# One encoder layer on one core: order of the first products, of RWKV's steps and of the attention's value transposes

## The chip, the cores and the metric

The kernel runs on one core of a Trainium2 chip. The metric is the time of one execution in microseconds of device time. The kernel before was run three times.

## The reference

One encoder layer over 512 tokens of 1024 channels, in float32:

```python
h = rms_norm(x, mix_norm_g)
proj = h @ w_in
y_a = short_conv_mixer(proj[SC])
y_b = stick_breaking_attention(q, k, v)
y_c = rwkv7_mixer(proj[RW])
y_d = spatial_gating(proj[SG])
gates = sigmoid(proj[GATE] + gate_b)
merged = sum over a, b, c, d of gate * (y @ out)
x = x + merged @ w_o
h = rms_norm(x, ffn_norm_g)
x = x + conv_glu_ffn(h, w_up, ffn_conv_w, w_down)
return rms_norm(x, final_norm_g)
```

RWKV needs, for each token and head, `kk / max(sqrt(sum(kk * kk)), 1e-12)` and a sum over `r * k * r_k`: two sums over the channels of a head. The attention has four heads of 64 with `z = q k / 8`, a causal mask, `log_sigmoid` and a suffix sum.

## The kernel before

Every large product is made of three matmuls (`mm3`, L168: lines 169, 170, 171), since each fp32 operand is held as a high part (a rounded cast) and a low part (the rest): high by high, low by high, high by low. Weights come from HBM in pieces of 128x512 (`load_piece`, L107 to L118), issued by SP. `split` (L99) makes ACT cast the high part `whi` (L100) and DVE subtract for the low part `wlo` (L101); for the first four pieces POOL subtracts. A unit (`col_unit`) is 256 columns of a weight, four pieces, 16 groups of three matmuls for all 512 tokens. PSUM has four banks with the tag "mm" for the products and four with the tag "wk" for everything else.

The program on TensorE, in order: the input's norm, whose scale is put on the diagonal of a matrix (L282) that multiplies x (L287); the first three units of w_in (columns RW0+768, then RW0+256 with RW0, then RW0+512), the first two in halves of 256 tokens (`gemm2_halves`, L341); the short convolution's columns, the gating unit's, RWKV's later work with gate columns; then q, k and v of the attention, the gates with the attention between them, the output products, and the FFN. ACT, DVE and TensorE take their instructions in a fixed order that is known when the kernel is built: in the first part ordered by hand, later by a scheduler, and it does not change at run time.

Side work is written as Python generators in four threads ("norm", "rw", "rw1", "sg"). After every group of three matmuls `mm3` calls `tick`, which lets each thread go on once its count has run out; `yield n` means to come back n groups later. The constants YA to YH, Y1, YS, WN, WN2 are such counts. `rwkv_half` (L397) runs in "rw" for the first two heads and in "rw1" for the others. Its steps that matter here: lora products (L420, L422); ACT's sigmoids; the scan `cs`; the gate product (L434) and the first head sum (`head_sum`, L416) of `sq`, whose result `ssm` (L441) goes through Ln (L448) and Exp (L449) on ACT; the head sum of `rk` after YA groups, whose parts `qH`, `qL` come from `split`; later the masks `Dm` (L541), built through a DRAM copy, and their first product (L552). The state step S is at L639 and L641. "sg" does the layer norm of the gating unit.

The attention: v is copied (`vT`, L906), transposed by TensorE in four pieces (L909), cast (`vS`, L914) and subtracted (L879). The generator `attention` then makes z in three "wk" banks (L932 to L934), and after Y1 groups issues Abs (L941), Exp (L942), Ln (L943), DVE's addition (L945) and `spH`, `spL`; YE groups later come the suffix sums (L953), Exp (L957), and YF groups later the products with vS (L965).

Of the kernel before, what the change touches and what calls it, by code (L numbers as in the profile page):

```python
# [31 lines left out]

YA, YB, YC, YD, YE, YF, YG, YH = 6, 16, 32, 20, 15, 5, 11, 3
Y1 = 3
YS = 2
WN = 19
WN2 = 5
ND = 3
# [10 lines left out]
def hybrid_encoder_layer(  # L49
# [44 lines left out]
    sp.dma_start(out=g_row, in_=mix_norm_g[0].rearrange("(k p) -> k p", p=P))  # L94
# [81 lines left out]

    def half_of(hf):
        return slice(512 * hf, 512 * hf + 512)
# [4 lines left out]
    def norm_factor(ss):  # L183
        s1 = small.tile([P, 1], F32, tag="s1", name="s1")
        vec.tensor_tensor(out=s1, in0=ss[:, 0:1], in1=ss[:, 1:2], op=ALU.add)
# [42 lines left out]

    def mix_stats(tt):
        ss, sq, _ = norm_start(npool)  # L230
        for hf in range(2):
            norm_sums(ss, x0[tt], sq, hf)
        mix_rs[tt] = norm_factor(ss)
# [8 lines left out]
    wslots[:] = [(npool, 4, 4)] * 4  # L242
    first = col_unit(w_in_v, RW0 + 768, get=load_piece)
    wslots[:] = [(wA, NRA, NWA)] * NWA
    u_first = [hl for _, hl in first]
    load_x(2)
    load_x(3)
    second = col_unit(w_in_v, RW0 + 256, RW0, get=load_piece)
    u_second = [hl for _, hl in second]

# [27 lines left out]
    with tc.manual_schedule(engines={mybir.EngineType.PE, mybir.EngineType.Activation, mybir.EngineType.DVE}):  # L278
        for tt in range(2):
            mix_stats(tt)  # L280
# [9 lines left out]
        s0 = mix_gain(0, 0)  # L290
        split(*first[0][0], pool)
        split(*first[1][0], pool)
        act.copy(s0[1], s0[0])
        s1 = mix_gain(1, 0)
        split(*first[2][0], pool)
        split(*first[3][0], pool)
        vec.tensor_tensor(out=s0[2], in0=s0[0], in1=s0[1].bitcast(F32), op=ALU.subtract)
        split(*s1)
        s0, s1 = mix_gain(0, 1), mix_gain(1, 1)
        split(*s0)  # L300
        split(*s1)
        for tt in range(2, 4):
            mix_stats(tt)
# [14 lines left out]
    spawn("norm", mix_rest())  # L318
    for raw_hi_lo, _ in second:
        split(*raw_hi_lo)  # L320

# [25 lines left out]

    def gemm2_halves(units, between):

        ps = [[bank(), bank()] for _ in units]  # L350
        for t2_ in range(2):
            t_ = slice(256 * t2_, 256 * t2_ + 256)
            for u, pu in zip(units, ps):
                for ci, kt in [(ci, kt) for h in range(4) for ci in range(2) for kt in range(2 * h, 2 * h + 2)]:
                    hi, lo = u[kt // 2]
                    cs = slice(ci * P, (ci + 1) * P)
                    mm3(pu[ci][:, t_], hi[:, kt % 2, cs], lo[:, kt % 2, cs], hH[:, kt, t_], hL[:, kt, t_], kt == 0, kt == KT - 1)
            if t2_ == 0:
                between()
        return ps  # L360
# [36 lines left out]
    def rwkv_half(j, lora, xg, zk, zr, zv):  # L397

        while j == 1 and stage[0] < 1:
            yield 1  # L400
# [30 lines left out]
        head_sum = parts_of(sq)  # L431
        yield 3
        pg = bank("wk")
# [242 lines left out]

    pz, pz2 = gemm2_halves([u_first, u_second], lambda: (finish("norm"), spawn("norm", turn_vectors())))
    finish("norm")
# [215 lines left out]
    for j in range(2):  # L894
        ps = pss2[j]
        ks = apool.tile([P, 2, T], F32R, tag="kS", name="kS", bufs=2)
        for hp in range(2):
            own, oth = HS[hp], HS[1 - hp]
            act.copy(ks[own, hp, :], ps[own, :])
            lo_of(ks[oth, hp, :], ps[own, :], ks[own, hp, :])  # L900
        kS.append(ks)
    pss2 = gemm2(col_unit(w_in_v, SB0 + 512))
    for j in range(2):
        ps = pss2[j]
        v = apool.tile([P, T], F32, tag="vT", name="vT", bufs=2)
        act.copy(v, ps)  # L906
        pt = bank("wk")
        for s in range(4):
            pe.transpose(out=pt[:, s * P:(s + 1) * P], in_=v[:, s * P:(s + 1) * P], identity=ident)  # L909
        vs = apool.tile([P, 2, NT, P], F32R, tag="vS", name="vS", bufs=2)  # L910
        for hp in range(2):
            own, oth = HS[hp], HS[1 - hp]
            src = pt.rearrange("p (s c) -> p s c", s=4)[:, :, own]
            act.copy(vs[:, hp, :, own], src)  # L914
            lo_of(vs[:, hp, :, oth], src, vs[:, hp, :, own])
        vS.append(vs)

# [232 lines left out]
```

## Time and profile before

| what | us |
|---|---|
| median of three runs | 870.81 |
| lowest, highest | 870.16, 874.03 |
| the profiled execution | 871.75 |
| its span in the trace | 870.0 |
| TensorE busy | 852.2 |
| DVE busy | 510.1 |
| ACT busy | 414.0 |
| POOL busy | 18.9 |
| mean granted clock of TensorE | 0.996 of full speed |

The sum of a prediction is made against the profiled execution, because all durations come from it. A wait in the list of waits is time in which the engine had its next instruction and could not start it.

### The profile page before, as it was taken

Reading aid. Unit: us, or ns where it says so; the run is one execution under the profiler, and the core shown is the slowest. Engines: PE = TensorE matmul, PEld = TensorE weight load, DVE = VectorE, ACT = ScalarE, POOL = GpSimd, SP = SyncE. Lnnn points to the kernel's source line nnn. Section 1 sums busy time; section 2 is a strip of 40 time slices with the busy share of each in tenths; the row PEclk is TensorE's granted clock in tenths of the full one; section 3 lists DMA queues with packets and bytes.
Section 4 is the critical chain, followed back from the end, with each engine's and each line's share of the span. In section 5 each row is a group of like instructions: output and inputs, shape, how many; then the busy total and the mean of one; then the engine's idle time right before and its main releaser. Section 6 shows DMA issues by size and latency. Waiting matters only on the chain.

```text
span 870.0 us, 12669 instructions
## 1 busy us (share of the span) xinstructions
PE 852.2 (98%) x4767; PEld 706.0 (81%) x4767; DVE 510.1 (59%) x872; ACT 414.0 (48%) x676; POOL 18.9 (2%) x61
## 2 busy tenths in 40 slices
PE   6999999999999999999999999999999999999997
PEld 6978877788778888888888888888888888888886
DVE  5577757875364655555556676635665366634645
ACT  6474344743343587774345554413444154412425
POOL 6000000000000000000000000000000000000000
PEclk9999999999999999999999999999999999999999
DMA  7233241134123322226338153313433063311102
GB/s 240 60 94 91 83 112 40 60 92 109 50 75 97 98 72 73 73 73 206 97 94 262 45 159 108 97 38 128 125 97 86 7 197 98 97 38 60 49 1 97
DMA packets 102773, 82.20 MB, mean 94 GB/s; under 512 B 12716, under 2 KB 92152, under 8 KB 102712
## 3 DMA queue, kind: packets, MB, share of 16 engines
q1 hardware_dynamic: 102040, 79.82, 30.8%
q10 hardware_dynamic: 592, 1.31, 0.4%
q8 instruction: 37, 0.61, 0.3%
q0 software_dynamic: 80, 0.26, 0.1%
q14 instruction: 24, 0.20, 0.1%
HBM read 78.88 MB, written 2.49 MB: 94 GB/s over the span
## 4 chain that ended last, share of the span: by engine, by line
PE 90%; DVE 3%; ACT 2%; DMA 2%; issue 1%; POOL 1%; POOLq 0%; ACTq 0%; SPq 0%
PE mm L169 25%; PE mm L171 24%; PE mm L170 24%; PE wk L171 3%; PE wk L170 3%; PE wk L169 3%; PE wk L552 1%; PE wk L953 1%; PE wk L965 1%; DMA raw<-in_w_down_dram 1%; PE wk L496 1%; ACT sq L181 0%; DVE ib L531 0%; DMA x<-in_x_dram 0%; POOL wlo L101 0%
## 5 line engine op out<-in xcount | busy, mean ns | idle before, releaser
L100 ACT CAST whi<-raw 128x512 fp32r<-128x512 f32 x276 | 168.9, 621 | 292.5 <-PE mm L170 168.2
L101 DVE TENSOR_TENSOR wlo<-raw,whi 128x512 fp32r<-128x512 f32 x272 | 185.3, 688 | 155.5 <-ACT whi L100 153.1
L169 PE MATMUL mm<-hH,whi 128*128 128x512 f32 (+1 forms) x448 | 173.8, 388 | 1.0 <-ACT hH L100 0.9
L171 PE MATMUL mm<-hH,wlo 128*128 128x512 f32 (+1 forms) x448 | 169.4, 378 | 3.6 <-POOL wlo L101 3.6
L170 PE MATMUL mm<-hL,whi 128*128 128x512 f32 (+1 forms) x448 | 169.1, 378 | 0.9 <-DVE hL L101 0.9
L169 PE MATMUL mm<-h2H,whi 128*128 128x512 f32 (+1 forms) x368 | 140.0, 381 | 0.6 <-ACT h2H L100 0.6
L170 PE MATMUL mm<-h2L,whi 128*128 128x512 f32 (+1 forms) x368 | 139.9, 380 | 0.5 <-DVE h2L L101 0.5
L171 PE MATMUL mm<-h2H,wlo 128*128 128x512 f32 (+1 forms) x368 | 139.8, 380 | 0.0
L171 PEld LDWEIGHTS mm<-hH,wlo 128*128 128x128 f32 x448 | 85.5, 191 | 19.4 <-POOL wlo L101 3.8
L169 PEld LDWEIGHTS mm<-hH,whi 128*128 128x128 f32 x448 | 85.5, 191 | 18.5 <-issue 1.5
L170 PEld LDWEIGHTS mm<-hL,whi 128*128 128x128 f32 x448 | 85.5, 191 | 15.0 <-DVE hL L101 1.3
L169 PEld LDWEIGHTS mm<-h2H,whi 128*128 128x128 f32 x368 | 69.2, 188 | 13.9 <-ACT h2H L100 0.8
L170 PEld LDWEIGHTS mm<-h2L,whi 128*128 128x128 f32 x368 | 69.2, 188 | 13.9 <-DVE h2L L101 0.7
L171 PEld LDWEIGHTS mm<-h2H,wlo 128*128 128x128 f32 x368 | 69.2, 188 | 13.0
L171 PE MATMUL mm<-whi,aL 128*128 128x512 f32 (+1 forms) x92 | 35.5, 386 | 0.0
L169 PE MATMUL mm<-whi,aH 128*128 128x512 f32 (+1 forms) x92 | 35.4, 385 | 0.0
L170 PE MATMUL mm<-wlo,aH 128*128 128x512 f32 (+1 forms) x92 | 35.4, 385 | 0.0
L171 PE MATMUL wk<-whi,aL 128*128 128x512 f32 (+1 forms) x88 | 33.8, 384 | 0.0
L170 PE MATMUL wk<-wlo,aH 128*128 128x512 f32 (+1 forms) x88 | 33.8, 384 | 0.0
L169 PE MATMUL wk<-whi,aH 128*128 128x512 f32 (+1 forms) x88 | 33.8, 384 | 0.0
L1063 DVE SCALAR_TENSOR_TENSOR ga<-mm,vecs,ga 128x511 f32<-128x511 f32 x22 | 16.5, 750 | 29.3 <-ACT ga L1062 29.3
L1031 DVE TENSOR_TENSOR xt<-xt,mm 128x512 f32<-128x512 f32 x16 | 11.0, 688 | 31.7 <-PE mm L171 31.7
(346 smaller groups left out, 1198.8 us busy)
## 6 DMA issues: line engine op xcount, KB each, us to landing
raw<-in_w_in_dram SPq DMA_DIRECT2D x104, 256.0 KB
raw<-in_w_up_dram SPq DMA_DIRECT2D x176, 128.0 KB
raw<-in_w_down_dram SPq DMA_DIRECT2D x44, 256.0 KB
raw<-in_w_o_dram SPq DMA_DIRECT2D x16, 256.0 KB
x<-in_x_dram SPq DMA_DIRECT2D x4, 512.0 KB
raw<-in_w_in_dram SPq DMA_DIRECT2D x16, 128.0 KB
xt<-in_x_dram SPq DMA_DIRECT2D x4, 512.0 KB
out_dram<-xn SPq DMA_DIRECT2D x4, 320.0 KB
```

The source lines that it names most:

```text
L100: act.copy(hi, src)
L101: eng.tensor_tensor(out=lo, in0=src, in1=hi.bitcast(F32), op=ALU.subtract)
L169: pe.matmul(ps, lhsT=sh, rhs=mh, start=first, stop=False)
L170: pe.matmul(ps, lhsT=sh, rhs=ml, start=False, stop=False)
L171: pe.matmul(ps, lhsT=sl, rhs=mh, start=False, stop=last)
L496: pe.matmul(pgs[hp][:, q * P:(q + 1) * P], lhsT=lt, rhs=rh, start=True, stop=True)
L552: pe.matmul(ps[us, i * 64:i * 64 + 64], lhsT=lt, rhs=rh, start=True, stop=True)
L953: pe.matmul(reg, lhsT=lt, rhs=s_[:, OFF[sj]:OFF[sj] + W[sj]], start=False, stop=(sj == 3 and n == 1), skip_group_check=True)
L965: pe.matmul(po[:, si * P:T], lhsT=vS[j][:, hp, si, :], rhs=a_[:, cols], start=(si == 0 and n == 0), stop=(si == 3 and n == 1))
L1031: vec.tensor_tensor(out=xt[:, tt, half_of(hf)], in0=xt[:, tt, half_of(hf)], in1=bk, op=ALU.add)
L1063: vec.scalar_tensor_tensor(out=t0[:, 1:T], in0=ps[:, 0:T - 1], scalar=ffc(1, i), in1=t0[:, 1:T], op0=ALU.mult, op1=ALU.add)
```

## The change

- g_row is loaded by a DMA on ACT's queue, ahead of x. The first norm squares a row tile of 1024 columns in one instruction.
- The low parts of the first four pieces are made by DVE in a written order; `split` has no engine argument any more.
- The loads are ordered: x tiles 0 and 1, the first unit, the upper half of the second unit's rows, x tile 2, the rest of the second unit, x tile 3, the third unit. The third unit joins the first two: all three for the first 256 tokens (the first two in quarters, the third on two "wk" banks), then all three for the second 256.
- `rwkv_half` of the first heads starts 8 groups later (Y0). YN (5, was 3) stands ahead of the gate product, YP (5, was 3) ahead of P2, YC is 36 for 32, YS 3 for 2, WN 20, WN2 10.
- The value transposes with their casts become a generator `turn_values` in thread "sg", spawned after the attention, that starts after YV = 4 groups.

```diff
-YA, YB, YC, YD, YE, YF, YG, YH = 6, 16, 32, 20, 15, 5, 11, 3
+YA, YB, YC, YD, YE, YF, YG, YH = 6, 16, 36, 20, 15, 5, 11, 3
 Y1 = 3
-YS = 2
-WN = 19
-WN2 = 5
+YS = 3
+YN = 5
+YV = 4
+YP = 5
+Y0 = 8
+WN = 20
+WN2 = 10
...
-    def split(src, hi, lo, eng=vec):
+    def lo_of(src, hi, lo):
+        vec.tensor_tensor(out=lo, in0=src, in1=hi.bitcast(F32), op=ALU.subtract)
+
+    def split(src, hi, lo):
         act.copy(hi, src)
-        eng.tensor_tensor(out=lo, in0=src, in1=hi.bitcast(F32), op=ALU.subtract)
+        lo_of(src, hi, lo)
...
-    load_x(2)
-    load_x(3)
-    second = col_unit(w_in_v, RW0 + 256, RW0, get=load_piece)
+    second = col_unit(w_in_v[:, 0:KT // 2], RW0 + 256, RW0, get=load_piece)
+    load_x(2)
+    second += col_unit(w_in_v[:, KT // 2:KT], RW0 + 256, RW0, get=load_piece)
+    load_x(3)
+    wslots[:] = [(npool, 8, 8)]
+    third = col_unit(w_in_v, RW0 + 512, get=load_piece)
...
+        s0 = mix_gain(0, 0)
+        act.copy(s0[1], s0[0])
+        lo_of(*w[0])
+        s1 = mix_gain(1, 0)
+        act.copy(s1[1], s1[0])
+        lo_of(s0[0], s0[1], s0[2])
+        lo_of(s1[0], s1[1], s1[2])
+        lo_of(*w[1])
+        ss2 = mix_sums(2)
+        split(*w[2])
+        split(*w[3])
...
+    def first_units():
+
+        u = [[hl for _, hl in w] for w in (first, second, third)]
+        ps = [[bank(), bank()], [bank(), bank()]]
+        for hs in ((0, 1), (2, 3)):
+            for n in range(2):
+                gemm2_part(u[n], ps[n], 0, hs)
+        finish("norm")
+        ps.append([bank("wk"), bank("wk")])
+        gemm2_part(u[2], ps[2], 0)
+        spawn("norm", turn_vectors())
+        for hs in ((0, 1), (2, 3)):
+            for n in range(3):
+                gemm2_part(u[n], ps[n], 1, hs)
         return ps
...
+    vT = []
     for j in range(2):
-        ps = pss2[j]
         v = apool.tile([P, T], F32, tag="vT", name="vT", bufs=2)
-        act.copy(v, ps)
-        pt = bank("wk")
...
+        act.copy(v, pss2[j])
+        vT.append(v)
+
+    def turn_values():
+        yield YV
+        for j in range(2):
+            pt = bank("wk")
+            for s in range(4):
+                pe.transpose(out=pt[:, s * P:(s + 1) * P], in_=vT[j][:, s * P:(s + 1) * P], identity=ident)
...
     spawn("rw", attention())
+    spawn("sg", turn_values())
```

In the changed kernel the lines are some tens further on: a cast of `split` is L110 and a subtraction L107; Ln and Exp of `ssm` are L493 and L494.

ACT round RWKV's first head sum, before (gT is the gate product's copy, `y` the tile that Ln and Exp write, qH the high part of rk):

```order
L444 ACTIVATE wp<-cs 128x8x64
L446 ACTIVATE wm<-cs 128x512
L436 COPY gT<-wk 128x512
L100 CAST qH<-rk 128x512
L448 ACT_TABLE_LOAD
L448 ACTIVATE y_772<-ssm 128x512
L100 CAST whi<-raw 128x512
L449 ACT_TABLE_LOAD
L449 ACTIVATE y_772<-y_772 128x512
```

The same in the changed kernel, where scb is a copy of the short convolution's columns:

```order
L517 COPY var<-zv 128x4x2x64
L481 COPY gT<-wk 128x512
L110 CAST whi<-raw 128x512
L493 ACT_TABLE_LOAD
L493 ACTIVATE y_838<-ssm 128x512
L797 COPY scb<-mm 128x512
L494 ACT_TABLE_LOAD
L494 ACTIVATE y_838<-y_838 128x512
L110 CAST qH<-rk 128x512
```

The cast qH<-rk stood ahead of both table loads and stands behind both now.

TensorE where the attention begins, before (L909 the value transposes, L932 to L934 the z products):

```order
L171 MATMUL mm<-hH,wlo 128x512
L909 MATMUL wk<-ident,vT 128x128 x8
L169 MATMUL mm<-hH,whi 128x512
L170 MATMUL mm<-hL,whi 128x512
L171 MATMUL mm<-hH,wlo 128x512
L932 MATMUL wk<-qS,kS 128x512
L933 MATMUL wk<-qL,kS 128x512
L934 MATMUL wk<-neg_r,ident_r 128x128
```

The same in the changed kernel, from the last group of three ahead of the transposes (L955); the z products (L978 to L980) stand four groups ahead:

```order
L181 MATMUL mm<-hH,wlo 128x512
L179 MATMUL mm<-hH,whi 128x512
L180 MATMUL mm<-hL,whi 128x512
L181 MATMUL mm<-hH,wlo 128x512
L955 MATMUL wk<-ident,vT 128x128 x8
L179 MATMUL mm<-hH,whi 128x512
```

All eight transposes stood one group ahead of z; they stand four groups behind z now, still in one run.

ACT there, before, from the second copy of v to spH (L941 Abs, L942 Exp, L943 Ln):

```order
L906 COPY vT<-mm 128x512
L914 CAST vS<-wk 128x4x64 x4
L941 ACTIVATE az<-wk 128x512
L941 ACTIVATE az<-wk 128x256
L941 ACTIVATE az<-wk 128x512
L942 ACT_TABLE_LOAD
L942 ACTIVATE az<-az 128x1280
L100 CAST whi<-raw 128x512
L943 ACT_TABLE_LOAD
L943 ACTIVATE az<-az 128x1280
L100 CAST whi<-raw 128x512
L100 CAST spH<-az 128x1280
```

The same in the changed kernel, from Abs (L987) on; L988 is Exp, L989 Ln, L960 the value casts:

```order
L987 ACTIVATE az<-wk 128x512
L987 ACTIVATE az<-wk 128x256
L987 ACTIVATE az<-wk 128x512
L988 ACT_TABLE_LOAD
L988 ACTIVATE az<-az 128x1280
L110 CAST whi<-raw 128x512
L989 ACT_TABLE_LOAD
L989 ACTIVATE az<-az 128x1280
L960 CAST vS<-wk 128x4x64
L110 CAST spH<-az 128x1280
L960 CAST vS<-wk 128x4x64 x3
```

The four value casts stood ahead of Abs; the first stands behind Ln now and the others behind spH. On DVE the subtraction that belongs to the first stands behind the three additions (L991), and the other three behind spL.

## Rows read from the trace of the kernel before

**Rows 1.** The page, part 1: engine, busy us (share of the span), instructions:
```profile
PE 852.2 (98%) x4767; PEld 706.0 (81%) x4767; DVE 510.1 (59%) x872; ACT 414.0 (48%) x676; POOL 18.9 (2%) x61
```

**Rows 2.** Waits of TensorE: line <- waited for: us in total, times, longest:
```profile
PE mm L171 <- POOL wlo L101: 3.6, 1, 3.6
PE wk L552 <- DVE Dm L541: 1.7, 1, 1.7
...
PE wk L909 <- ACT vT L906: 0.6, 1, 0.6
PE wk L639 <- DVE S L641: 0.5, 1, 0.5
...
PE wk L416 <- DVE qL L101: 0.2, 1, 0.2
```

**Rows 3.** Timeline of TensorE at the start: start, us, line, operation:
```profile
13.50 0.38 PE L170 MATMUL mm<-hL,whi 128*128 128x256 f32 x1 [0.92 <-DVE hL L101]
...
20.55 0.58 PE L171 MATMUL mm<-hH,wlo 128*128 128x256 f32 x1 [3.61 <-POOL wlo L101]
...
26.04 0.30 PE L169 MATMUL mm<-hH,whi 128*128 128x256 f32 x1
...
27.03 0.28 PE L171 MATMUL mm<-hH,wlo 128*128 128x256 f32 x1
```

**Rows 4.** Windows of 1 us: PE, PEld, DVE, ACT, POOL busy, PEclk, DMA share, GB/s:
```profile
20.00:21.00 1.00, 0.46 (x2) 0.46 (x3) 0.22 (x1) 0.75 (x4) 1.00 (x2) 0.50 1.06 328
```

**Rows 5.** Timeline of POOL and DVE at the start:
```profile
19.23 2.50 POOL L101 TENSOR_TENSOR wlo<-raw,whi 128x512 fp32r<-128x512 f32 x2
...
11.05 1.76 DVE L297 TENSOR_TENSOR hL<-hf,hH 128x512 fp32r<-128x512 f32 x1
12.73 0.72 DVE L101 TENSOR_TENSOR hL<-hf,hH 128x512 fp32r<-128x512 f32 x1
```

**Rows 6.** Timeline of ACT at the start: a cast that waited for its DMA:
```profile
12.95 0.62 ACT L100 CAST whi<-raw 128x512 fp32r<-128x512 f32 x1 [0.81 <-DMA raw<-in_w_in_dram]
```

**Rows 7.** Timeline of TensorE, DVE and ACT round the second head sum:
```profile
60.04 0.79 PE L416 MATMUL wk<-qH,hones_r 128*128 128x512 f32 x1
...
65.02 0.39 PE L416 MATMUL wk<-qH,hones_r 128*128 128x512 f32 x1
65.25 0.39 PE L416 MATMUL wk<-qL,hones_r 128*128 128x512 f32 x1
...
62.16 0.69 DVE L441 TENSOR_SCALAR ssm<-wk 128x512 f32<-128x512 f32 x1
...
62.92 1.28 ACT L448 ACT_TABLE_LOAD   x1 [0.57 <-DVE ssm L441]
64.22 0.63 ACT L448 ACTIVATE y<-ssm 128x512 f32<-128x512 f32 x1
...
65.38 1.28 ACT L449 ACT_TABLE_LOAD   x1
```

**Rows 8.** Timeline of TensorE, ACT and DVE at the attention's first pass:
```profile
307.02 0.39 PE L932 MATMUL wk<-qS,kS 128*128 128x512 f32 x1
...
311.48 0.39 PE L169 MATMUL mm<-hH,whi 128*128 128x512 f32 x1
...
305.67 0.38 ACT L914 CAST vS<-wk 128x256 fp32r<-128x256 f32 x1
...
313.87 1.27 ACT L943 ACTIVATE az<-az 128x1280 f32<-128x1280 f32 x1
...
316.89 1.27 ACT L100 CAST spH<-az 128x1280 fp32r<-128x1280 f32 x1 [1.24 <-DVE az L945]
...
306.08 0.42 DVE L879 TENSOR_TENSOR vS<-wk,vS 128x256 fp32r<-128x256 f32 x1
...
315.18 1.62 DVE L945 SCALAR_TENSOR_TENSOR az<-wk,az 128x512 f32<-128x512 f32 x3 [1.89 <-ACT az L943]
...
318.19 1.49 DVE L101 TENSOR_TENSOR spL<-az,spH 128x1280 fp32r<-128x1280 f32 x1 [0.79 <-ACT spH L100]
```

More of the change, by code (lines that the diff above doesn't have):

```diff
@@ L73, in bank, with half_of @@
         return psum.tile([P, 512], F32, tag=tag, name=tag, bufs=4)
+    def half_of(hf):
+        return slice(512 * hf, 512 * hf + 512)
     npool, nst = open_pool("npool", "right")
@@ L81, in hybrid_encoder_layer @@
     g_row = npool.tile([KT, P], F32, name="g_row")
+    act.dma_start(out=g_row, in_=mix_norm_g[0].rearrange("(k p) -> k p", p=P))
     eps = const.tile([P, 1], F32, name="eps")
@@ L175, in hybrid_encoder_layer, with norm_factor @@
     hL = hpool.tile([P, KT, T], F32R, tag="hL", name="hL")
-    def half_of(hf):
-        return slice(512 * hf, 512 * hf + 512)
     def norm_sums(ss, xs, sq, hf):
         act.activation(out=sq[:, half_of(hf)], in_=xs[:, half_of(hf)], func=AF.Square, accum_out=ss[:, hf:hf + 1])
-    def norm_factor(ss):
-        s1 = small.tile([P, 1], F32, tag="s1", name="s1")
-        vec.tensor_tensor(out=s1, in0=ss[:, 0:1], in1=ss[:, 1:2], op=ALU.add)
+    def norm_factor(ss, parts=2):
+        s1 = ss[:, 0:1]
+        if parts == 2:
+            s1 = small.tile([P, 1], F32, tag="s1", name="s1")
+            vec.tensor_tensor(out=s1, in0=ss[:, 0:1], in1=ss[:, 1:2], op=ALU.add)
         rt = small.tile([P, 1], F32, tag="rt", name="rt")
@@ L227, in hybrid_encoder_layer, with mix_sums, mix_factor @@
     mix_rs, mix_pt = {}, {}
-    def mix_stats(tt):
+    def mix_sums(tt):
         ss, sq, _ = norm_start(npool)
-        for hf in range(2):
-            norm_sums(ss, x0[tt], sq, hf)
-        mix_rs[tt] = norm_factor(ss)
+        act.activation(out=sq, in_=x0[tt], func=AF.Square, accum_out=ss[:, 0:1])
+        return ss
+    def mix_factor(tt, ss):
+        mix_rs[tt] = norm_factor(ss, 1)
     def mix_gain(tt, half):
@@ L240, in mix_gain @@
         return hf_, hH[:, half * 4:half * 4 + 4, tt * P:(tt + 1) * P], hL[:, half * 4:half * 4 + 4, tt * P:(tt + 1) * P]
-    wslots[:] = [(npool, 4, 4)] * 4
+    wslots[:] = [(npool, 8, 8)]
     first = col_unit(w_in_v, RW0 + 768, get=load_piece)
-    wslots[:] = [(wA, NRA, NWA)] * NWA
-    u_first = [hl for _, hl in first]
-    load_x(2)
-    load_x(3)
-    second = col_unit(w_in_v, RW0 + 256, RW0, get=load_piece)
-    u_second = [hl for _, hl in second]
+    wslots[:] = [(wA, NRA, NWA)]
+    second = col_unit(w_in_v[:, 0:KT // 2], RW0 + 256, RW0, get=load_piece)
+    load_x(2)
+    second += col_unit(w_in_v[:, KT // 2:KT], RW0 + 256, RW0, get=load_piece)
+    load_x(3)
+    wslots[:] = [(npool, 8, 8)]
+    third = col_unit(w_in_v, RW0 + 512, get=load_piece)
+    wslots[:] = [(wA, NRA, NWA)] * NWA
     rows = {}
@@ L279, in hybrid_encoder_layer @@
         for tt in range(2):
-            mix_stats(tt)
+            mix_factor(tt, mix_sums(tt))
             dg = npool.tile([P, P], F32, tag="diag", name="diag", bufs=2)
@@ L289, in hybrid_encoder_layer, with mix_norm @@
         mix_xn = {}
[L290 to L303, printed above, removed]
+        def mix_norm(tt, ss):
+            mix_factor(tt, ss)
             mix_xn[tt] = npool.tile([P, D], F32, tag="xn", name="xn", bufs=2)
             act.mul(mix_xn[tt], x0[tt], mix_rs[tt])
+        w = [raw_hi_lo for raw_hi_lo, _ in (first[0], first[1], second[0], second[1], first[2], first[3], second[2], second[3])]
+        for n in range(2):
+            act.copy(w[n][1], w[n][0])
+        s0 = mix_gain(0, 0)
[9 more added lines that the diff above has]
+        split(*w[3])
+        for n in (4, 5):
+            act.copy(w[n][1], w[n][0])
+        s0, s1 = mix_gain(0, 1), mix_gain(1, 1)
+        act.copy(s0[1], s0[0])
+        act.copy(s1[1], s1[0])
+        lo_of(s0[0], s0[1], s0[2])
+        lo_of(s1[0], s1[1], s1[2])
+        lo_of(*w[4])
+        lo_of(*w[5])
+        mix_norm(2, ss2)
+        split(*w[6])
+        split(*w[7])
+        mix_norm(3, mix_sums(3))
+        for raw_hi_lo, _ in third:
+            split(*raw_hi_lo)
     def mix_rest():
@@ L318, in hybrid_encoder_layer @@
     spawn("norm", mix_rest())
-    for raw_hi_lo, _ in second:
-        split(*raw_hi_lo)
     vecs = const.tile([P, 2 * P], F32, name="vecs")
@@ L346, in gemm2, with gemm2_part @@
         return ps
[L348 to L359, printed above, removed]
+    def gemm2_part(u, ps, t2_, hs=range(4)):
+        t_ = slice(256 * t2_, 256 * t2_ + 256)
+        for ci, kt in [(ci, kt) for h in hs for ci in range(2) for kt in range(2 * h, 2 * h + 2)]:
+            hi, lo = u[kt // 2]
+            cs = slice(ci * P, (ci + 1) * P)
+            mm3(ps[ci][:, t_], hi[:, kt % 2, cs], lo[:, kt % 2, cs], hH[:, kt, t_], hL[:, kt, t_], kt == 0, kt == KT - 1)
+    def first_units():
+        u = [[hl for _, hl in w] for w in (first, second, third)]
+        ps = [[bank(), bank()], [bank(), bank()]]
+        for hs in ((0, 1), (2, 3)):
+            for n in range(2):
+                gemm2_part(u[n], ps[n], 0, hs)
[6 more added lines that the diff above has]
+                gemm2_part(u[n], ps[n], 1, hs)
         return ps
@@ L397, in rwkv_half @@
     def rwkv_half(j, lora, xg, zk, zr, zv):
+        if j == 0:
+            yield Y0
         while j == 1 and stage[0] < 1:
@@ L431, in rwkv_half @@
         head_sum = parts_of(sq)
-        yield 3
+        yield YN
         pg = bank("wk")
@@ L675, in rwkv_half @@
         y_split("c", j, yc)
-    pz, pz2 = gemm2_halves([u_first, u_second], lambda: (finish("norm"), spawn("norm", turn_vectors())))
+    pz, pz2, pz3 = first_units()
     finish("norm")
@@ L876, in hybrid_encoder_layer @@
     qS, qL, kS, vS = [], [], [], []
-    def lo_of(out, src, hi):
-        vec.tensor_tensor(out=out, in0=src, in1=hi.bitcast(F32), op=ALU.subtract)
     pss2 = gemm2(col_unit(w_in_v, SB0))
@@ L899, in hybrid_encoder_layer @@
             act.copy(ks[own, hp, :], ps[own, :])
-            lo_of(ks[oth, hp, :], ps[own, :], ks[own, hp, :])
+            lo_of(ps[own, :], ks[own, hp, :], ks[oth, hp, :])
         kS.append(ks)
     pss2 = gemm2(col_unit(w_in_v, SB0 + 512))
+    vT = []
     for j in range(2):
-        ps = pss2[j]
         v = apool.tile([P, T], F32, tag="vT", name="vT", bufs=2)
-        act.copy(v, ps)
-        pt = bank("wk")
[L908 to L916, printed above, removed]
+        act.copy(v, pss2[j])
[6 more added lines that the diff above has]
+                pe.transpose(out=pt[:, s * P:(s + 1) * P], in_=vT[j][:, s * P:(s + 1) * P], identity=ident)
+            vs = apool.tile([P, 2, NT, P], F32R, tag="vS", name="vS", bufs=2)
+            for hp in range(2):
+                own, oth = HS[hp], HS[1 - hp]
+                src = pt.rearrange("p (s c) -> p s c", s=4)[:, :, own]
+                act.copy(vs[:, hp, :, own], src)
+                lo_of(src, vs[:, hp, :, own], vs[:, hp, :, oth])
+            vS.append(vs)
     OFF = [0, 512, 1024, 896]
@@ L1068, in up_pair @@
         u = col_unit(w_up_v, i * P, DFF + i * P)
-        pu = gemm2_halves([u], lambda: finish("norm"))[0] if i == 0 else gemm2(u)
+        if i == 0:
+            pu = [bank(), bank()]
+            gemm2_part(u, pu, 0)
+            finish("norm")
+            gemm2_part(u, pu, 1)
+        else:
+            pu = gemm2(u)
         ga = conv(pu[0], i, "ga")
```

6 lines of the change are left out of this document (2 added, 4 removed).

## Prediction

> **What bounds the kernel now.** I read the page first, then the list of TensorE's waits, then the timelines of the few places that this list names. The page gives TensorE 852.2 of 870.0 us [rows 1]: it is the bound from end to end, and a change elsewhere counts only where it shortens or makes a wait of TensorE, or changes its clock. The list of waits is short, and four of its rows stand at places that this change edits: 3.6 us for POOL's low part of a weight, 1.7 for Dm, 0.5 for S, 0.2 for qL [rows 2]. The start costs more than its wait. The first product with hL starts at 13.50, the stall ends at 20.55, and the 26 matmuls from there to 26.04 are 0.211 us apart, where the next eight of the same width, to 27.03, are 0.124 apart [rows 3]. The granted clock explains it: 0.50 after the stall, that is 1.2 in place of 2.4 GHz [rows 4]. So 26 x (0.211 - 0.124) = 2.3 us went with the clock that fell after a 3.6 us pause. After the pause of 1.7 for Dm I saw no such spacing.
>
> **The first products (gain).** Low parts of the first four weight pieces leave POOL, which takes 1.25 us for one (2.50 for two, at 19.23, where TensorE waits); beside it one DVE subtraction took 1.76 us, where its like took 0.72 [rows 5]. In the new order DVE makes them as they are needed. That removes the 3.6 us wait and its 2.3 us of half clock. hL comes earlier by 1.04 (1.76 - 0.72) and by about 0.3 for the single Square that saves an add and a small instruction ahead of the diagonal: 1.35. Against it: the third unit is now run in half-width pairs, 16 groups of three products, each as six matmuls 0.12 apart [rows 3] where it was three 0.23 apart (65.02, 65.25) [rows 7]: +0.4. And x tile 2 and the later weight pieces come behind more bytes. ACT already waited 0.81 for such a piece [rows 6]; in the new order ACT's Square of tile 2 stands ahead of casts that TensorE needs, and the two late row tiles have to be normalised before the third unit ends its first half. I take three small waits, 1.35 together, from that row (one of 0.6, two of 0.35 to 0.4), between 0 and 3.5. The sum is -3.6 - 2.3 - 1.35 + 0.4 + 1.35 = **-5.5**, between -6.9 and -3.4.
>
> **The small waits (gain).** Dm's consumer is issued ten groups later (YC 36 for 32, and the third unit ahead of it), some 6.9 us at 0.69 each, against a wait of 1.7: gone. S (YS 3) and qL: 0.7 gone. In the attention, the second vT copy (0.6) [rows 2] was waited for because the transposes followed it at once; four groups and the z products now lie between. Together **-3.0**. The layer-norm chain of the gating unit comes to stand behind Dm and weights on DVE, and its consumer waits: I take +0.6, nearest to the 0.5 of S, between 0 and the 1.7 of Dm.
>
> **The second head sum of the first RWKV half (loss).** Its wait now is 0.2. Six groups lie between the first head sum's start (60.04) and the second's (65.02), and YA, which sets that, stays 6. What has changed is ACT's order between them, in the first order fence: rk's high part was cast ahead of the table load of Ln, now it comes behind table load, Ln, a copy, table load and Exp. These need ssm, which started 2.1 us behind the first head sum's start (62.16) [rows 7]. From ssm's start: 0.76 to the table load, 1.30 to Ln, 1.16 to the next load (a copy between, as a cast is now), 1.30 to Exp, then 0.6 for Exp and 0.7 for the cast (a 512-wide cast takes 0.62 [rows 6]) and 0.7 for DVE's qL (ssm, of the same width, takes 0.69): 6.5 us. TensorE comes to the second head sum's qL 4.98 + 0.23 = 5.2 us after the first's start. So it waits 2.1 + 6.5 - 5.2 = 3.4, and with ssm behind two more DVE instructions (the mixing of three units is now bunched ahead of it) up to 4.6. I take **+3.8**, between 2.2 and 5.0. What is queued behind it is all of TensorE's work.
>
> One rule here speaks for less, another for more. The rows show a table load of 1.28 and Ln 0.02 us behind its end (62.92 + 1.28, 64.22) [rows 7]. The Trainium skill (ScalarE: Activation LUTs, What ACT_TABLE_LOAD costs) puts 1.38 us of drain on top of every switch; the sum would be 5.5 us higher for the four loads of the two new chains. Its section Table sets: the hidden batching unit has Ln and Exp in one set, with a single load; that would take 1.28 off each chain, but the order rows of the changed kernel keep a load between Ln and Exp, so the trace's price for two loads is the one used.
>
> **The value transposes (loss).** Before, they stood ahead of the z products, with four "wk" PSUM banks free. Now z holds three of the four, and both groups of four transposes take the one that is left. So the second group waits until the copies out of the first are done: two casts on ACT and two subtractions on DVE. The last two order fences show ACT: the first cast comes behind Abs, Exp, Ln and their loads, the second behind spH. On DVE the first subtraction comes behind the three additions, the second behind spL. Counted from the first z product (307.02 before): z and four groups end 4.46 later (311.48), the first four transposes take about 0.5 more, so TensorE is at the second group at +5.0. Ln ends at 313.87 + 1.27, at +8.1; the first cast (0.38) goes then. The three additions on DVE (1.62, from 315.18) end at +9.8; the casts of spH (1.27, from 316.89) at +11.1; the second value cast at +11.5; spL (1.49, from 318.19) at +12.7; the last subtraction (0.42) at +13.1 [rows 8]. The wait is 13.1 - 5.0 = **+8.1**. Its bounds are 7.5 (the weight cast between the two table loads costs nothing) and 9.0 (that cast waits 0.8 for its DMA, as in [rows 6]). TensorE's order is fixed, so nothing runs past it.
>
> **The clock.** Both new pauses are longer than the 3.6 us after which the clock fell, so I take 2.3 us for each, **+4.6**; the nearest row without a fall is the 1.7 us pause for Dm, so each is between 0 and 3.
>
> **The sum.** Gains -5.5 - 3.0 = -8.5; losses 3.8 + 8.1 + 0.6 + 4.6 = 17.1. The profiled execution took 871.75 us (span 870.0), so 880.35 in its terms; it stands 0.94 above the median of the runs, 870.81, so **879.4 us**. Everything from the attention's end on is issued as before and counts nothing: there TensorE's own order and its buffers set the pace.
>
> **Rivals.** (1) Only the attention pause is real: rk's chain comes early enough, since ACT and DVE have idle time in which the mixing may be done before the first head sum. Then neither its 3.8 nor its 2.3 is there: 870.81 - 8.5 + 8.1 + 2.3 + 0.6 = 873.3. For it: the mixing of two units can begin before the three units end. Against it: ssm has to wait for the first head sum in any case, and from there on the chain alone gives 2.2 at the least.
> (2) Faster: the second group of transposes is held back only by something long done, because its bank is another or because z's banks come free sooner. Then ACT's order costs nothing there, no clock is lost, and the head sum costs its lower bound: 870.81 - 8.5 + 2.2 + 0.6 = 865.1. It decides at a wait of about 1.5 us or less. For it: tile buffers are handed out by a scheduler and not by the text. Against it: in the order rows the second group is a long run behind the z products, whose three banks are read until the last Exp of that pass.
> (3) The change does not do what it says at the start: the second unit's pieces now come ahead of tile 2 of x, and a wait for tile 2 of some 2 us takes the place of the old one, with another fall of the clock. The start then gains 5.5 - 2.0 - 2.3 = 1.2 in place of 5.5: 883.7. For it: transfers fill the first 14 us, and ACT did wait for one. Against: 0.8 was the longest of these waits.
> (4) By the skill's drain on each table load: 879.4 + 5.5 = 884.9. No load in the rows shows it.
>
> **Chances.** Forecast 0.60 (by itself 875.5 to 883), rival 1 0.17, rival 2 0.10, rival 3 0.10, rival 4 0.03. A difference within 0.5%, 4.35 us, is what a measurement of this kernel can't tell from none. Slower by more: forecast, rivals 3 and 4, less 0.03 of the forecast's lower end: 0.70. Within: rival 1 and that 0.03: 0.20. Faster: 0.10. The range of 866.0 to 884.5 takes in rival 1 and most of rival 3 and leaves out rival 2 and rival 4.
>
> **What would show it.** In the changed profile the wait for POOL is gone and the first three units end some 5 to 6 us sooner; the waits of TensorE are led by the transposes on the DVE subtraction of vS with about 8 us, then the head sum on qH or qL with 3 to 5; the clock row reads 0.5 for some 5 us behind each. If the transposes' wait is under 2 us, the forecast is wrong by its largest term; if the clock stays at 1.0 behind the pauses, by up to 4.6; if the head sum's wait is under 1, rival 1 holds.

## The result, and the profile after

| | before | changed |
|---|---|---|
| median, us | 870.47 (6 runs) | 877.33 (6 runs) |
| lowest, highest | 869.76, 874.03 | 876.20, 877.74 |
| the profiled execution, its span | 871.75, 870.0 | 876.39, 874.7 |
| mean granted clock | 0.996 | 0.992 |

The ratio is 1.0071 with an interval of 1.0053 to 1.0089: slower by 6.9 us. The forecast was 879.4 us, slower.

The waits of TensorE in the changed kernel answer to [rows 2]. A row gives the line, what it waited for, us in total, times, and the longest:

```profile
PE wk L955 <- DVE vS L107: 8.1, 1, 8.1
PE wk L461 <- ACT qH L110: 3.0, 1, 3.0
...
PE mm L179 <- DVE hf L249: 1.2, 1, 1.2
...
PE wk L861 <- DVE uv L856: 0.4, 1, 0.4
```

The rows for POOL, Dm, S and vT are gone. Two new ones lead, at the two places the prediction named: 8.1 us at the value transposes (L955) and 3.0 at the second head sum (L461), with 0.2 more for its low part. The third, for hf (the normalised input), belongs to the start.

The start, to be read with [rows 3] (TensorE's timeline; in brackets the idle time ahead of the instruction and what ended it):

```profile
11.79 0.38 PE L180 MATMUL mm<-hL,whi 128*128 128x256 f32 x1 [0.34 <-DVE hL L107]
...
15.83 0.35 PE L179 MATMUL mm<-hH,whi 128*128 128x256 f32 x1 [1.17 <-DVE hf L249]
...
55.20 0.69 PE L465 MATMUL wk<-lora,w2a 64*128 64x512 f32 x1
```

The first product with hL starts at 11.79 where it started at 13.50, and no pause is longer than 1.17 us. The lora product (L465) comes 57 groups into the program, at 55.20; before, the same product (L420) came after 49 groups, at 56.34. With 8 groups at 0.685 us the start has won 56.34 + 5.5 - 55.20 = 6.6 us.

Round the second head sum, to be read with [rows 7] (TensorE, DVE, ACT):

```profile
60.26 0.79 PE L461 MATMUL wk<-qH,hones_r 128*128 128x512 f32 x1
...
68.38 0.51 PE L461 MATMUL wk<-qH,hones_r 128*128 128x512 f32 x1 [2.98 <-ACT qH L110]
69.11 0.80 PE L461 MATMUL wk<-qL,hones_r 128*128 128x512 f32 x1 [0.22 <-DVE qL L107]
...
62.72 0.69 DVE L486 TENSOR_SCALAR ssm<-wk 128x512 f32<-128x512 f32 x1
...
63.48 1.28 ACT L493 ACT_TABLE_LOAD   x1 [0.40 <-DVE ssm L486]
64.78 0.63 ACT L493 ACTIVATE y<-ssm 128x512 f32<-128x512 f32 x1
...
65.90 1.28 ACT L494 ACT_TABLE_LOAD   x1
67.19 0.63 ACT L494 ACTIVATE y<-y 128x512 f32<-128x512 f32 x1
67.73 0.60 ACT L110 CAST qH<-rk 128x512 fp32r<-128x512 f32 x1
```

DVE's ssm starts 2.46 us behind the first head sum. From there ACT goes through table load, Ln, a copy, table load and Exp before it casts rk's high part at 67.73. TensorE, free since about 65.4, gets it at 68.38 and the low part at 69.11.

At the attention's first pass, to be read with [rows 8] (TensorE, ACT, DVE):

```profile
301.42 0.39 PE L978 MATMUL wk<-qS,kS 128*128 128x512 f32 x1
...
305.88 0.60 PE L955 MATMUL wk<-ident,vT 128*128 128x128 f32 x4
314.57 1.08 PE L955 MATMUL wk<-ident,vT 128*128 128x128 f32 x4 [8.09 <-DVE vS L107]
...
308.27 1.27 ACT L989 ACTIVATE az<-az 128x1280 f32<-128x1280 f32 x1
309.45 0.35 ACT L960 CAST vS<-wk 128x256 fp32r<-128x256 f32 x1
311.30 1.26 ACT L110 CAST spH<-az 128x1280 fp32r<-128x1280 f32 x1 [1.50 <-DVE az L991]
312.47 0.36 ACT L960 CAST vS<-wk 128x256 fp32r<-128x256 f32 x1
...
309.57 1.62 DVE L991 SCALAR_TENSOR_TENSOR az<-wk,az 128x512 f32<-128x512 f32 x3 [1.89 <-ACT az L989]
311.11 0.41 DVE L107 TENSOR_TENSOR vS<-wk,vS 128x256 fp32r<-128x256 f32 x1
312.59 1.49 DVE L107 TENSOR_TENSOR spL<-az,spH 128x1280 fp32r<-128x1280 f32 x1 [1.07 <-ACT spH L110]
314.00 0.42 DVE L107 TENSOR_TENSOR vS<-wk,vS 128x256 fp32r<-128x256 f32 x1
```

Between the two groups of transposes (305.88 and 314.57) stand Ln, the first value cast, the additions, spH, the second value cast, spL and the last subtraction, which ends at 314.42, 13.0 us behind the first z product. TensorE does nothing in this time.

The clock behind each pause (windows of 1 us; behind the window its length, the busy time of PE, PEld, DVE, ACT and POOL, the granted clock, the DMA share, GB/s):

```profile
68.00:69.00 1.00, 0.51 (x1) 0.19 (x1) 0.64 (x2) 1.00 (x3) 0.00 (x0) 1.00 0.04 14
70.00:71.00 1.00, 1.00 (x4) 0.72 (x4) 1.00 (x3) 0.00 (x0) 0.00 (x0) 0.50 0.39 53
73.00:74.00 1.00, 1.00 (x7) 0.80 (x6) 0.93 (x2) 0.27 (x1) 0.00 (x0) 1.00 0.00 0
...
312.00:313.00 1.00, 0.00 (x0) 0.00 (x0) 0.41 (x1) 0.83 (x2) 0.00 (x0) 0.50 0.00 0
317.00:318.00 1.00, 1.00 (x3) 0.72 (x3) 0.38 (x1) 0.00 (x0) 0.00 (x0) 0.50 0.00 0
319.00:320.00 1.00, 1.00 (x6) 0.78 (x6) 0.55 (x1) 0.42 (x1) 0.00 (x0) 1.00 0.00 0
```

It falls to 0.50 0.7 us behind the first pause (at 69.1) and 3.1 us ahead of the end of the second (at 311.4), and is back at 1.00 some 4 us after TensorE has gone on. At 0.50 products of 128x512 start 0.427 us apart, at 1.00 0.227. So half of the time that TensorE works at 0.50 is counted as lost: 1.7 us from 69.1 to 72.5 and 1.85 from 314.6 to 318.3.

### The profile page after: what moved, and what is told of

Read it like the earlier page. It is cut to its first block, busy times and chain, and to the rows that moved or that the text cites. A ratio compares the mean times of both kernels' runs of the same rounds, so it can differ in the third digit from the quotient of the medians.

```text
span 874.7 us, 12733 instructions
## 1 busy us (share of the span) xinstructions
PE 852.4 (97%) x4815; PEld 707.0 (81%) x4815; DVE 510.5 (58%) x872; ACT 412.9 (47%) x669; POOL 11.4 (1%) x57
## 4 chain that ended last, share of the span: by engine, by line
PE 92%; ACT 3%; DMA 2%; DVE 2%; issue 1%; SPq 0%; ACTq 0%
PE mm L179 25%; PE mm L181 25%; PE mm L180 25%; PE wk L181 3%; PE wk L180 3%; PE wk L179 3%; PE wk L597 1%; PE wk L999 1%; DMA raw<-in_w_down_dram 1%; DMA x<-in_x_dram 1%; PE wk L1011 1%; DMA raw<-in_w_in_dram 1%; PE wk L541 0%; PE wk L567 0%; PE wk L684 0%
## 5 line engine op out<-in xcount | busy, mean ns | idle before, releaser
L110 ACT CAST whi<-raw 128x512 fp32r<-128x512 f32 x272 | 165.9, 621 | 304.8 <-PE mm L180 179.6
L107 DVE TENSOR_TENSOR wlo<-raw,whi 128x512 fp32r<-128x512 f32 x276 | 187.4, 689 | 170.4 <-ACT whi L110 170.2
L179 PE MATMUL mm<-hH,whi 128*128 128x512 f32 (+1 forms) x432 | 167.9, 389 | 1.8 <-DVE hf L249 1.2
L180 PE MATMUL mm<-hL,whi 128*128 128x512 f32 (+1 forms) x432 | 162.7, 377 | 0.3 <-DVE hL L107 0.3
L181 PE MATMUL mm<-hH,wlo 128*128 128x512 f32 (+1 forms) x432 | 162.8, 377 | 0.0
L179 PEld LDWEIGHTS mm<-hH,whi 128*128 128x128 f32 x432 | 82.2, 190 | 19.2 <-issue 1.5
L181 PEld LDWEIGHTS mm<-hH,wlo 128*128 128x128 f32 x432 | 81.8, 189 | 15.2
L180 PEld LDWEIGHTS mm<-hL,whi 128*128 128x128 f32 x432 | 82.2, 190 | 14.0 <-DVE hL L107 0.5
L179 PEld LDWEIGHTS mm<-h2H,whi 128*128 128x128 f32 x368 | 69.2, 188 | 13.1
```

Of the source, the lines that this page charges most:

```text
L107: vec.tensor_tensor(out=lo, in0=src, in1=hi.bitcast(F32), op=ALU.subtract)
L179: pe.matmul(ps, lhsT=sh, rhs=mh, start=first, stop=False)
L180: pe.matmul(ps, lhsT=sh, rhs=ml, start=False, stop=False)
L181: pe.matmul(ps, lhsT=sl, rhs=mh, start=False, stop=last)
```

## The experiments

All times are medians; in each run the kernel before was timed on the same chip (870.5 to 870.8 us).

### The value transposes ahead of z again

```diff
     for j in range(2):
         v = apool.tile([P, T], F32, tag="vT", name="vT", bufs=2)
         act.copy(v, pss2[j])
-        vT.append(v)
+        pt = bank("wk")
+        for s in range(4):
+            pe.transpose(out=pt[:, s * P:(s + 1) * P], in_=v[:, s * P:(s + 1) * P], identity=ident)
...
-    spawn("sg", turn_values())
```

> The changed kernel (877.3 us, trace: wait of 8.1 us at the value transposes, then about 4 us at half clock) with the value transposes and their copies put back ahead of the z products, nothing else. If that one wait and its clock are what the move cost: 8.1 of wait and 1.8 of clock go, the wait of 0.6 for the second vT copy returns: about 868.0 us, clock 1.00 from 300 to 320. Rival, that the attention's first pass is late for another reason (ACT has too much to do there) and the wait only shows where: the time stays above 873, with the wait now in front of the suffix sums.

Measured 867.64 us, ratio to before 0.9963 (0.9951 to 0.9976). The 8.1 us wait is gone, the one of 0.6 us for vT is back, the clock reads 1.00 from 300 to 320, and no wait appears at the suffix sums. So the pass itself is not late; the place of the transposes is.

### The two groups of transposes apart

```diff
             vS.append(vs)
+            yield 27
```

> The changed kernel with the value transposes where they are, but the second group of four issued 27 groups after the first, when the one free bank has long been emptied. If the reuse of that bank is the cause: no wait over 0.5 us at the transposes, about 877.3 - 8.1 - 1.8 = 867.4 us, a little under the run with the transposes ahead of z. If it is ACT's order as such (value casts behind Ln and spH), the wait stays or moves to the products with vS and the time stays above 873.

Measured 866.85 us, 0.9947 (0.9927 to 0.9966), without any wait at the transposes. ACT's order is as it was: casts behind Ln and spH. That order costs nothing as long as nobody needs the bank, so the reuse of the one free bank is the cause, as the prediction had it. 10.5 us are won; the wait and its clock make 9.9.

### The second head sum later, at the cost of YC

```diff
-        yield YA
+        yield YA + (7 if j == 0 else 0)
...
-        yield YC
+        yield YC - (7 if j == 0 else 0)
```

> The changed kernel with the second head sum of the first RWKV half issued 13 groups after the first, in place of 6, and YC 7 less for that half, so that what follows keeps its place. If the wait of 3.2 us there and 1.7 us of half clock behind it are lost time: about 877.3 - 4.9 = 872.4 us. If TensorE only waits there for what it would wait for later (kkn and the masks behind the same chain): the wait comes back further on, and the time stays within 1.5 us of 877.3.

Measured 879.48 us, 1.0093 (1.0065 to 1.0120): slower than the changed kernel by 2. My expectation failed. The waits of TensorE:

```profile
PE wk L861 <- DVE uv L856: 4.9, 1, 4.9
PE wk L597 <- DVE Dm L586: 2.1, 1, 2.1
```

The head sum waits no more. But seven groups more ahead of the products from which Dm is made (`MT`, L541 in this kernel), taken out of the count behind them, made Dm late by 2.1 us, and the gating product (L861), whose layer norm stands behind Dm on DVE, by 4.9.

### Both of these edits

> Both of these edits together: second group of value transposes 27 groups later, second head sum 7 groups later. If the two pauses with their clock are the whole loss of the change and add up: 877.3 - 9.9 - 4.9 = 862.5 us, faster than the kernel before by 8. If they overlap or the waits move on: 866 or more.

Measured 868.70 us, 0.9974 (0.9960 to 0.9988). This is the second expectation: the transposes' part is won, the rest lost at the same two places. TensorE, and the clock round it:

```profile
122.74 1.15 PE L597 MATMUL wk<-Dm,AoT 64*64 64x64 f32 x32 [2.68 <-DVE Dm L586]
...
129.63 2.90 PE L861 MATMUL wk<-uv,wsT 128*128 128x256 f32 x6 [4.85 <-DVE uv L856]
```

```profile
121.00:122.00 1.00, 0.00 (x0) 0.00 (x0) 0.10 (x1) 0.00 (x0) 0.00 (x0) 1.00 0.55 52
130.00:131.00 1.00, 1.00 (x3) 0.78 (x3) 0.23 (x2) 0.00 (x0) 0.00 (x0) 0.50 0.00 0
```

### The second head sum later, at the cost of YB

```diff
-        yield YA
+        yield YA + (7 if j == 0 else 0)
...
-        yield YB
+        yield YB - (7 if j == 0 else 0)
```

> The changed kernel with the second head sum of the first half again 7 groups later, but the 7 groups are now taken out of YB (the count behind it), so that the mask products, Dm and its DRAM copy keep their place. The run before this one took them out of YC, behind the mask products, and so pushed Dm and the layer norm behind it on DVE back by 7 groups; that is how I read its waits at Dm (2.1) and at the gating product (4.9). If so: no wait over 0.6 at head sum or Dm, and 877.3 - 4.9 = 872.4 us. Rival, that whatever is saved at the head sum is lost at the gating product, because DVE's layer norm is late by itself: a wait of 3 us or more there, and the time stays above 875.

Measured 871.51 us, 1.0006 (0.9996 to 1.0017): 5.8 us less than the changed kernel, where 4.9 was expected. There is no wait at the head sum or at Dm, and 0.4 at the gating product. So the wait at the head sum was lost time of its own, and what failed in the earlier pair was the place from which the seven groups were taken.

### Both pauses out

> That edit and the second group of value transposes 27 groups later together. If both pauses with their clock are the whole loss: 866.85 (transposes apart alone) - 4.9 = 862.0 us, below the kernel before by 8.5; under the rival 865 or more.

Measured 861.26 us, 0.9894 (0.9880 to 0.9909): faster than the kernel before by 9.6 us and than the changed one by 16. The longest waits left are small:

```profile
PE wk L233 <- DVE ones_f L87: 1.3, 1, 1.3
PE mm L179 <- DVE hf L249: 1.1, 1, 1.1
```

The first of them is the wait for the matrix of ones at the very beginning, as before. The two pauses with their clock are the whole loss of the change, and they add up: 10.5 and 5.8 us singly, 16.1 together. That is 1.2 more than the waits and the half clock in the changed kernel's one profile (8.1 + 1.85 + 3.2 + 1.7); where it lies is not shown.

### The low parts of the first unit on POOL again

```diff
+    def lo_of(src, hi, lo, eng=vec):
...
+        lo_of(*w[0], pool)
...
+        lo_of(*w[1], pool)
...
+        lo_of(*w[4], pool)
+        lo_of(*w[5], pool)
```

> The changed kernel with only the low parts of the first unit's four pieces back on POOL. If these made the start of the kernel before slow: POOL's third and fourth come behind its masks again, TensorE waits 3 to 4 us for them, the clock falls behind that for some 5 us: 877.3 + 3.5 + 2 = about 883 us. If the order of loads and the joined third unit made the gain and POOL's part would be hidden there: within 1.5 us of 877.3.

Measured 880.03 us, 1.0111 (1.0094 to 1.0128): 2.7 us more than the changed kernel, between the two expectations. POOL's third and fourth low parts, and TensorE's wait for the third:

```profile
20.09 3.00 POOL L107 TENSOR_TENSOR wlo<-raw,whi 128x512 fp32r<-128x512 f32 x2
...
21.46 0.39 PE L181 MATMUL mm<-hH,wlo 128*128 128x256 f32 x1 [2.20 <-POOL wlo L107]
```

```profile
22.00:23.00 1.00, 1.00 (x10) 0.91 (x8) 0.00 (x0) 0.00 (x0) 1.00 (x1) 1.00 1.02 344
```

POOL is as late as it was before (20.09 here, 19.23 in [rows 5]), but TensorE now has the second unit's upper rows to do first; it comes later (at 19.26, where it came at 16.94), waits 2.2 us in place of 3.6, and the clock does not fall.

### The pause filled with products by zero

```diff
             vS.append(vs)
+            for _ in range(34 if j == 0 else 0):
+                pe.matmul(now[0], lhsT=zero_r, rhs=hH[:, 0, :], start=False, stop=False)
```

Here `now` holds the bank of the sum that runs, and `zero_r` a matrix of zeros.

> The changed kernel with 34 products of 128x512 by a matrix of zeros (added into the sum that runs) ahead of the second group of value transposes: 34 x 0.228 = 7.75 us of TensorE's work inside the pause of 8.1 us. It adds no time as long as the pause is there for another reason. If the fall of the clock behind the pause comes from TensorE standing still: the clock reads 1.00 through 306 to 320, the wait is 0.3 or so, and 1.8 us are won: 875.5 us. If the clock falls for another reason, or not: 877.3.

Measured 875.92 us, 1.0065 (1.0050 to 1.0080): 1.4 us less than the changed kernel although TensorE does 34 products more. The filling and the second group of transposes:

```profile
306.88 7.98 PE L971 MATMUL mm<-hH,zero_r 128*128 128x512 f32 x34
315.23 0.63 PE L962 MATMUL wk<-ident,vT 128*128 128x128 f32 x4 [0.38 <-DVE vS L107]
```

```profile
316.00:317.00 1.00, 1.00 (x6) 0.82 (x5) 0.42 (x1) 0.51 (x2) 0.00 (x0) 1.00 0.00 0
```

The clock stays at 1.00 where it read 0.50, so its fall came from TensorE standing still. The price is less certain: the medians give 1.4 us, the windows gave 1.85, but this run's interval (1.0050 to 1.0080) and that of the changed kernel (1.0053 to 1.0089) overlap.

### The first two units each as a whole

```diff
-        for hs in ((0, 1), (2, 3)):
-            for n in range(2):
-                gemm2_part(u[n], ps[n], 0, hs)
+        for n in range(2):
+            gemm2_part(u[n], ps[n], 0)
```

This edit and the two that follow start from the kernel with both pauses out.

> The fastest kernel so far (861.26 us: changed kernel with both pauses taken out) with one part of the start undone: on the first 256 tokens the first unit is run through all its rows before the second, as in the kernel before, in place of quarters in turn. With low parts from DVE, the lower rows' hL and low parts are there at 17 to 19 us by the changed kernel's trace, and TensorE would come for them at 14.7. If the turn-taking covers that: a pause of 2 to 3 us in one or two pieces at the hH, hL or wlo of the first unit, in place of the 1.1 us wait on hf, and 861.3 + 1.5 = 862.8 us with the clock at 1.00. Rival, that it makes no difference because the start is set by when x and the weights land: within 0.5 of 861.3.

Measured 865.48 us, 0.9940 (0.9924 to 0.9957): 4.2 us more than with the units in turn. TensorE and its clock:

```profile
17.39 0.38 PE L179 MATMUL mm<-hH,whi 128*128 128x256 f32 x1 [2.56 <-ACT hH L330]
```

```profile
21.00:22.00 1.00, 1.00 (x6) 1.00 (x6) 0.93 (x2) 1.00 (x3) 0.00 (x0) 0.50 0.01 1
```

The pause is 2.6 us (0.35 and 0.2 more behind it), as expected; that the clock would fall behind it was not, and adds 1.7. The edit changes TensorE's order alone. ACT and DVE still prepare the second unit's upper rows first: ACT casts these from 13.55 to 14.67 and comes to the hH for which TensorE waits only then:

```profile
16.72 0.62 ACT L330 CAST hH<-hf 128x512 fp32r<-128x512 f32 x1
```

In the kernel before, ACT had made both lower hH by 15.75. So this run shows what it costs when TensorE's order does not fit ACT's, and not what the kernel before's whole order would cost with low parts from DVE; that was not run.

### YC and YS as before

```diff
-YA, YB, YC, YD, YE, YF, YG, YH = 6, 16, 36, 20, 15, 5, 11, 3
+YA, YB, YC, YD, YE, YF, YG, YH = 6, 16, 32, 20, 15, 5, 11, 3
...
-YS = 3
+YS = 2
```

> The fastest kernel so far with YC and YS back at their old values, 32 and 2. The prediction gave the longer YC and the longer YS the end of the waits for Dm (1.7) and S (0.5). If the later start of the first RWKV half and the joined third unit already freed Dm's chain on DVE: no wait for Dm, only that for S is back, 861.3 + 0.5 = 861.8 us. If the count YC was what removed it: a wait of 1 to 2 us at Dm's first product and 862.8 or more.

Measured 861.44 us, 0.9899 (0.9884 to 0.9913): no different. Dm is not waited for, and S for 0.2 us, in place of 0.5.

### The banks of the second and third unit exchanged

```diff
-        ps = [[bank(), bank()], [bank(), bank()]]
+        ps = [[bank(), bank()], [bank("wk"), bank("wk")]]
...
-        ps.append([bank("wk"), bank("wk")])
+        ps.append([bank(), bank()])
```

> The fastest kernel so far with the PSUM banks of the second and third first units exchanged (the second on the two wk banks), so that the second does not wait for DVE to empty a bank of the norm (1.1 us). By the changed kernel's trace the next needs stand close behind: hL of the lower rows is 0.2 late then, and the transposes of the third row tile's xn 0.7. So if waits in a row cover each other: 861.3 - 0.3 = 861.0 us, with the wait now on xn or hL. If the 1.1 us is lost time by itself: 860.2 us.

Measured 861.18 us, 0.9895 (0.9880 to 0.9910). The wait for hf is gone and the time is the same within its interval, as the first expectation has it. The trace bears it out: the first product with hL of the first rows starts at 12.17 (12.02 with the banks as they were), then TensorE waits 0.17 for hL and 0.22 for a low part, and the transposes of the third row tile start at 20.78, where they started at 20.72. So nearly all of the 1.1 us was covered by the next needs. The wait on the first diagonal, 1.2 us in this profile, costs little: the product that waits starts at 7.06, and at 6.88 there, without a wait, because the products ahead of it ended later.

## Why the prediction was right

| term | predicted | in the trace |
|---|---|---|
| first products | -5.5 | -6.6 |
| Dm, S, vT, qL | -3.0 | -2.8 and the 0.2 of qL, which stays |
| gating product | +0.6 | +0.4 |
| second head sum | +3.8 | +3.2 less the 0.2 there was |
| value transposes | +8.1 | +8.1 |
| clock | +4.6 | 1.7 + 1.85 = 3.5 |
| sum | +8.6 | +5.6 |

The spans differ by 4.7, so 0.9 us of gain is not in these terms. Of it 0.7 stands where the prediction counted nothing, at the first products of the FFN: they wait 0.61 and 0.46 us for their input's high and low part in the kernel before, and 0.38 in the changed one. That code is the same in both, and in the other profiles this wait is 0.2 to 0.8 us, so it changes from one execution to the next.

Each term that was off by more than 0.2 us made the forecast too slow, and that 879.4 came within 2.1 us of the median is in part luck. Profile against profile the change costs 4.6 us (876.39 less 871.75), where 8.6 was worked out. But the profiled execution of the changed kernel lies 0.9 below its median and that of the kernel before 1.3 above its own, so that the medians differ by 6.9.

**The value transposes.** Right in mechanism and size: TensorE was through the first group at +5.1 (305.88 + 0.60, from 301.42) and went on at +13.15; +5.0 and +13.1 were worked out. A wait of 8.1 us rules out rival 2, which decided at 1.5 us or less, and the two ways of giving the bank back (transposes ahead of z, or apart) both took the loss away.

**The head sum.** Right in place and cause. ssm started 2.46 us behind the first head sum, inside the span assumed (2.1 to 3.3); from ssm's start to the product with qL it took 6.39 us (62.72 to 69.11), where 6.5 was worked out. The list of waits counts from the modelled end of the product ahead, the prediction from start to start; by starts the loss is 3.6. Rival 1, that this part is covered, did not happen: 5.8 us came back when the wait was taken away. The first experiment on it misled: it showed that the time of such a wait can be lost again by moving the wrong count. That was my edit's fault and not the prediction's.

**The clock.** The mechanism was right, the size was off: 2.3 us each was taken from the one fall in the kernel before; 1.7 and 1.85 were measured. (Counted as these are, that one fall cost 2.8.) The changed kernel's clock was back after some 4 us, and not 5.5. But this price is not a constant. In the run with the transposes ahead of z the same pause of 2.98 us stands ahead of the head sum; TensorE went on at 69.09, and the clock was back at 75.2 only, 3.05 us lost:

```profile
74.00:75.00 1.00, 1.00 (x4) 0.81 (x3) 0.64 (x2) 0.00 (x0) 0.00 (x0) 0.50 0.00 0
```

The reason that was given fits only one of the two pauses: both were to be longer than the 3.6 us behind which the clock fell before. The one at the head sum was 2.98, and the clock fell all the same; that it would was inside the stated range (0 to 3), not worked out.

**The first products.** The size was 1.1 too small. The first product with hL came 1.71 us earlier (13.50, 11.79), where 1.35 was worked out, the new wait was 1.17 in place of 1.35, and the clock's part is 2.8 in place of 2.3 if it is counted as above. One step of the working was wrong: it gave the whole pause of 3.6 and the clock's part to the low parts leaving POOL. With these back on POOL the loss is 2.7 only, because TensorE has the second unit's upper rows to do meanwhile. So the order of the units has a share in the gain; how large it would be by itself is not shown. The small waits that were to come from x tile 2 did come, 1.17 us in one piece. On ACT and DVE of the changed kernel:

```profile
12.10 1.06 ACT L240 ACTIVATE sq<-x 128x1024 f32<-128x1024 f32 x1 [1.09 <-DMA x<-in_x_dram]
...
13.15 1.13 ACT L110 CAST whi<-raw 128x512 fp32r<-128x512 f32 x2
...
13.79 1.29 DVE L107 TENSOR_TENSOR wlo<-raw,whi 128x512 fp32r<-128x512 f32 x2 [1.46 <-ACT whi L110]
15.00 1.28 DVE L249 TENSOR_TENSOR hf<-mm,gT_mix 128x512 f32<-128x512 f32 x2
```

ACT's Square of tile 2 waits 1.09 for its DMA; behind it the casts, DVE's subtractions, and at 15.00 hf, which empties the bank for which TensorE waits until 15.83. Rival 3, a wait of some 2 us with a fall of the clock at this place, came true in part in two other profiles with the same start (transposes apart, and the filled pause): there Square waited 2.2 and 2.1 us for its DMA and TensorE 2.2 for hf, but the clock stayed at 1.00. So the gain at the start is up to 1.1 us smaller from one execution to the next.

**The small waits.** They went, but not for the reason given: with YC at 32 and YS at 2 no wait for Dm returns, and 0.2 of the 0.5 for S. The prediction had Dm's first product come ten groups later, by YC and by the third unit ahead of it. The third unit stands ahead of the RWKV half in both kernels. The product comes 14 groups later (138 groups into the program, 124 before): 4 by YC, and 10 by Y0 and YN, which move the making of Dm back as well. What the trace shows in place of that reason is on DVE, where the many small steps on `ib` lead to Dm. Their first and their last, in the kernel before:

```profile
94.33 0.14 DVE L531 TENSOR_TENSOR ib<-ib 64x1 f32<-64x1 f32 x1
...
111.21 0.38 DVE L534 COPY ib<-ib 64x256 f32<-64x256 f32 x1
```

And in the changed kernel:

```profile
100.27 0.15 DVE L576 TENSOR_TENSOR ib<-ib 64x1 f32<-64x1 f32 x1
...
111.40 0.37 DVE L579 COPY ib<-ib 64x256 f32<-64x256 f32 x1
```

They took 17.3 us and take 11.5 now. Before, eight of DVE's instructions for the short convolution (5.6 us together) stood between these steps; now all eight stand ahead of the first. With YC and YS at their old values the steps take 11.6 us, so these two counts did not do it. The later start of the first half (Y0, YN) is what remains; it was not tried alone.

**Rival 4** falls with the rows: the table load at 63.48 takes 1.28 and Ln starts at 64.78, 0.02 us behind its end. The Trainium skill (ScalarE: Activation LUTs, What ACT_TABLE_LOAD costs) adds 1.38 us of drain for each switch; the trace shows none here.

## What to carry to other kernels

Where side work goes into the last free PSUM bank twice in a row, the time of the second use is set by the slowest copy out of the first, and that is read from the order on the copying engines, not from their load: DVE was busy for 59% of the span and ACT for 48% [rows 1]. Issue the second use when the bank has long been empty. And when a step is moved away from a wait, take the groups from a count whose slack is known; the same seven groups won 5.8 us when taken ahead of the mask products and lost 2.2 when taken behind them.

## What was not expected of the hardware

The length of a pause alone does not say whether the clock falls. It fell in or soon behind pauses of 2.6 us (units whole, at 15 to 17), 3.0 (the head sum), 4.85 and 8.1; it did not behind 2.1 and 2.7 (Dm, in the two runs with YC shortened) and 2.2 (POOL, and twice hf). The 2.7 that kept the clock (121 to 122 in the run with both edits) and the 2.6 that lost it are nearly alike. Nor does the length say what a fall costs: 1.7 us in one profile and 3.05 in another behind the same 2.98.
